# A row softmax on one core: the first of eight stores is issued from GpSimd instead of the Scalar engine

## The chip, the core and the metric

The kernel runs on one core of a Trainium2 chip. The metric is the device time of one execution in microseconds. Of the core's engines the kernel uses the vector engine (DVE), the scalar engine (ACT) and the queue of the sync engine (SP), which issues the loads. GpSimd (POOL) does only four small memsets at the start. Transfers between the chip's memory and the core's on-chip memory run on 16 DMA engines.

## The reference

The input is 16 x 1024 rows of 512 float32 values, 33.55 MB. Each row gets a softmax at temperature 0.5:

```python
temp = 0.5
x_scaled = x / temp
x_max = np.max(x_scaled, axis=-1, keepdims=True)
exp_x = np.exp(x_scaled - x_max)
return (exp_x / np.sum(exp_x, axis=-1, keepdims=True)).astype(np.float32)
```

The output has the same size, so 67.1 MB are moved in all.

## The kernel before

**Tiles.** The 16,384 rows are cut into 8 tiles (`c` = 0 to 7) of 128 partitions x 16 rows x 512 values, 4 MB each. The tile stays in place: it is loaded into an `xt` buffer, the exponentials and the scaled rows are written over it, and it is stored from there. There are 6 buffers (`BUFS`), so tiles 6 and 7 reuse those of tiles 0 and 1, and their loads wait until the stores of tiles 0 and 1 have landed.

**Blocks.** The work goes in blocks of rows of one tile: tile 0 has three (4, 4 and 8 rows), tiles 1 to 6 have one of 16 rows, tile 7 has two of 8. That makes 11 blocks, numbered 0 to 10.

**Steps of a block.**

- `shift` (loads L66, L74, L78): the tile's load is issued on SP's queue if that has not been done; DVE takes the negated maximum of each row (L74) and doubles it (L78) into `bias`.
- `exponentials` (L85): ACT computes exp(2x + bias) row by row and accumulates each row's sum.
- `scale_vector` (L100, L102): DVE takes the reciprocals of the sums and multiplies all but the last eighth of the block's rows.
- `scale_scalar` (L111): ACT scales the last eighth, one or two rows (none in the blocks of 4).
- `store` (L119): when the block is the last of its tile, one DMA of the whole tile, 4 MB, is issued.

**Order.** The schedule is written out by hand; every engine takes its instructions in the order of the program. The main loop runs over the blocks:

```python
shift(0)
shift(1)
exponentials(0)
for i in range(n):
    if i + 1 < n:
        exponentials(i + 1)
    scale_vector(i)
    scale_scalar(i)
    if i + 2 < n:
        shift(i + 2)
    store(i)
```

So on ACT the exponentials of the next block stand ahead of the last rows of this one, and the store's issue comes after both. All eight stores are issued on ACT's queue, and each waits for DVE's and ACT's rows of its tile. A new tile's load is issued within `shift`, in the order of tiles, on SP's queue; the load of tile 0 is split in two (1 MB and 3 MB).

Of the kernel before, what the change touches and what calls it, by code (L numbers as in the profile page):

```python
# [1 line left out]

# [4 lines left out]


@with_exitstack
def kernel(  # L10
    ctx: ExitStack,
    tc: tile.TileContext,
    x: bass.AP,
    out: bass.AP,
):
    nc = tc.nc
    fp32 = mybir.dt.float32
    P = nc.NUM_PARTITIONS
    AX = mybir.AxisListType.X
    EXP = mybir.ActivationFunctionType.Exp  # L20
    COPY = mybir.ActivationFunctionType.Copy
    MAX = mybir.AluOpType.max

    D = x.shape[-1]
    xf = x.flatten_outer_dims()
    of = out.flatten_outer_dims()
    N = xf.shape[0]

    G = 16
    C = N // (P * G)
    assert C * P * G == N
    xr = xf.rearrange("(c p g) d -> c p g d", p=P, g=G)
    outr = of.rearrange("(c p g) d -> c p g d", p=P, g=G)
    WHOLE = [(0, G)]
    LOADS = [[(0, 4), (4, G)]] + [WHOLE] * 7
    BLOCKS = [[(0, 4), (4, 8), (8, G)]] + [WHOLE] * 6 + [[(0, 8), (8, G)]]
    STORES = [WHOLE] * 8  # L40
    BMAX = 16
    BUFS = 6

    data = ctx.enter_context(tc.tile_pool(name="data", bufs=BUFS))
    stats = ctx.enter_context(tc.tile_pool(name="stats", bufs=6))

    ctx.enter_context(tc.manual_schedule())


    warm = stats.tile([P, 1], fp32, name="warm", bufs=1)  # L50
    nc.vector.memset(warm, 0.0)  # L51
    nc.scalar.activation(out=warm, in_=warm, func=EXP)  # L52

    chunks = {}
    blocks = [(c, lo, hi) for c in range(C) for lo, hi in BLOCKS[c]]
    n = len(blocks)
    biases, sums, recips = {}, {}, {}

    def load(c):
        if c < BUFS:  # L60
            chunks[c] = data.tile([P, G, D], fp32, name="xt")
        else:
            chunks[c] = chunks[c - BUFS]
        xt = chunks[c]
        for lo, hi in LOADS[c]:
            nc.sync.dma_start(out=xt[:, lo:hi, :], in_=xr[c][:, lo:hi, :])  # L66

    def shift(i):
        c, lo, hi = blocks[i]
        if c not in chunks:  # L70
            load(c)
        b = hi - lo
        negmax = stats.tile([P, BMAX], fp32, name="negmax")
        nc.vector.tensor_reduce(  # L74
            negmax[:, 0:b], chunks[c][:, lo:hi, :], axis=AX, op=MAX, negate=True
        )
        biases[i] = stats.tile([P, BMAX], fp32, name="bias")
        nc.vector.tensor_scalar_mul(biases[i][:, 0:b], negmax[:, 0:b], 2.0)  # L78

    def exponentials(i):  # L80
        c, lo, hi = blocks[i]
        sums[i] = stats.tile([P, BMAX], fp32, name="sums")
        for g in range(hi - lo):
            row = chunks[c][:, lo + g, :]
            nc.scalar.activation(  # L85
                out=row,
                in_=row,
                func=EXP,
                bias=biases[i][:, g : g + 1],
                scale=2.0,  # L90
                accum_out=sums[i][:, g : g + 1],
            )


    def scale_vector(i):
        c, lo, hi = blocks[i]
        b = hi - lo
        k = b - b // 8
        recips[i] = stats.tile([P, BMAX], fp32, name="recip")
        nc.vector.reciprocal(recips[i][:, 0:b], sums[i][:, 0:b])  # L100
        rows = chunks[c][:, lo : lo + k, :]
        nc.vector.tensor_mul(  # L102
            rows, rows, recips[i][:, 0:k].unsqueeze(2).broadcast_to((P, k, D))
        )

    def scale_scalar(i):
        c, lo, hi = blocks[i]
        b = hi - lo
        for g in range(b - b // 8, b):
            row = chunks[c][:, lo + g, :]  # L110
            nc.scalar.activation(  # L111
                out=row, in_=row, func=COPY, scale=recips[i][:, g : g + 1]
            )

    def store(i):
        c, _, end = blocks[i]
        for lo, hi in STORES[c]:
            if hi == end:
                nc.scalar.dma_start(  # L119
                    out=outr[c][:, lo:hi, :], in_=chunks[c][:, lo:hi, :]  # L120
                )

    shift(0)
    shift(1)
# [11 lines that stand above are left out]
# [1 line left out]
_INS = ['x']  # L137
_OUTS = [((16, 1024, 512), 'float32')]


# [23 lines left out]
```

## Time and profile before

| what | value |
|---|---|
| median of 4 runs | 162.4 us (162.32 to 162.69) |
| the profiled execution's own time | 162.43 us |
| its span, first to last instruction | 160.7 us |
| DVE busy | 134.6 us (84%) |
| ACT busy | 102.1 us (64%) |
| POOL busy | 0.2 us, four memsets |
| bytes moved | 67.13 MB, mean 418 GB/s |
| store, issue to landing | 12.4 to 32.4 us, median 22.9 |
| load of 4 MB, median issue to landing | 30.0 us |

The span is what the profiler saw of the program's instructions; the rest of the execution's time lies before and after it. Times inside the profile count from the start of the span. "L74" is line 74 of the kernel file. In the rows of busy tenths, the span is cut into 40 slices of 4 us, and a digit is the busy share of a slice. The page's q1 is the queue of the loads (issued by SP) and q10 that of the stores (issued by ACT). "ACTq" and "SPq" are those engines' queues of issues, which are not counted as busy time. An issue only starts a transfer; the landing is when its data has arrived.

### The profile page before, as it was taken

Reading aid. Unit: us, or ns where it says so; the run is one execution under the profiler, and the core shown is the slowest. Engines: PE = TensorE matmul, PEld = TensorE weight load, DVE = VectorE, ACT = ScalarE, POOL = GpSimd, SP = SyncE. Lnnn points to the kernel's source line nnn. Section 1 sums busy time; section 2 is a strip of 40 time slices with the busy share of each in tenths; the row PEclk is TensorE's granted clock in tenths of the full one; section 3 lists DMA queues with packets and bytes.
Section 4 is the critical chain, followed back from the end, with each engine's and each line's share of the span. In section 5 each row is a group of like instructions: output and inputs, shape, how many; then the busy total and the mean of one; then the engine's idle time right before and its main releaser. Section 6 shows DMA issues by size and latency. Waiting matters only on the chain.

```text
span 160.7 us, 402 instructions
## 1 busy us (share of the span) xinstructions
DVE 134.6 (84%) x45; ACT 102.1 (64%) x273; POOL 0.2 (0%) x4
## 2 busy tenths in 40 slices
DVE  0608999999999999999999999999999999956000
ACT  3072549069979963997299909990999890790000
POOL 0000000000000000000000000000000000000000
DMA  5999999999999999999999999999999999999993
GB/s 196 457 457 457 392 424 490 392 400 508 392 400 392 392 498 408 400 465 441 400 457 449 400 441 467 392 441 473 392 408 506 392 392 514 400 392 514 400 392 139
DMA packets 2450, 67.13 MB, mean 418 GB/s; under 512 B 272, under 2 KB 272, under 8 KB 272
## 3 DMA queue, kind: packets, MB, share of 16 engines
q1 hardware_dynamic: 1296, 33.56, 49.2%
q10 hardware_dynamic: 1152, 33.55, 48.4%
q14 instruction: 2, 0.02, 0.0%
HBM read 33.55 MB, written 33.55 MB: 418 GB/s over the span
## 4 chain that ended last, share of the span: by engine, by line
DVE 80%; DMA 7%; ACT 4%; issue 0%; SPq 0%
DVE negmax L74 42%; DVE xt L102 36%; DMA xt<-in_x_dram 7%; ACT xt L85 4%; DVE bias L78 1%; DVE recip L100 1%; SPq L66 0%
## 5 line engine op out<-in xcount | busy, mean ns | idle before, releaser
L85 ACT ACTIVATE xt<-xt,bias 128x512 f32<-128x512 f32 x128 | 90.4, 707 | 41.6 <-DVE bias L78 41.1
L74 DVE TENSOR_REDUCE negmax<-xt 128x16 f32<-128x8192 f32 (+2 forms) x11 | 69.9, 6352 | 9.4 <-DMA xt<-in_x_dram 9.4
L102 DVE TENSOR_TENSOR xt<-xt,recip 128x7168 f32<-128x7168 f32 (+2 forms) x11 | 62.0, 5637 | 0.4
L85 ACT ACTIVATION_READ_ACCUMULATOR xt<-xt,bias 128x1 f32 x128 | 23.9, 186 | 0.0
L111 ACT ACTIVATE xt<-xt,recip 128x512 f32<-128x512 f32 x15 | 9.9, 705 | 0.0
L100 DVE RECIPROCAL recip<-sums 128x16 f32<-128x16 f32 (+2 forms) x11 | 2.4, 218 | 1.8 <-ACT xt L85 1.8
L78 DVE TENSOR_SCALAR bias<-negmax 128x16 f32<-128x16 f32 (+2 forms) x11 | 1.9, 173 | 0.4
L52 ACT ACT_TABLE_LOAD x1 | 1.3, 1283 | 0.7 <-PEq L148 0.7
L51 DVE MEMSET warm<- 128x1 f32 x1 | 0.1, 59 | 0.8 <-PEq L148 0.8
L52 ACT ACTIVATE warm<-warm 128x1 f32<-128x1 f32 x1 | 0.2, 203 | 0.0
L148 POOL MEMSET const-uint8-127<- 128x1 uint8 x1 | 0.1, 103 | 0.0
L148 POOL MEMSET const-bfloat16-1.0<- 128x1 bf16 x1 | 0.1, 102 | 0.0
L148 POOL MEMSET const-float32-0.0<- 128x1 f32 x1 | 0.1, 99 | 0.2 <-issue 0.2
L148 POOL MEMSET const-float32-1.0<- 128x1 f32 x1 | 0.1, 99 | 0.0
## 6 DMA issues: line engine op xcount, KB each, us to landing
out_dram<-xt ACTq DMA_DIRECT2D x8, 4096.0 KB, 22.9
xt<-in_x_dram SPq DMA_DIRECT2D x7, 4096.0 KB, 30.0
xt<-in_x_dram SPq DMA_DIRECT2D x1, 3072.0 KB, 11.6
xt<-in_x_dram SPq DMA_DIRECT2D x1, 1024.0 KB, 4.7
```

Source lines behind the costliest of these rows:

```text
L51: nc.vector.memset(warm, 0.0)
L52: nc.scalar.activation(out=warm, in_=warm, func=EXP)
L74: nc.vector.tensor_reduce(negmax[:, 0:b], chunks[c][:, lo:hi, :], axis=AX, op=MAX, negate=True)
L78: nc.vector.tensor_scalar_mul(biases[i][:, 0:b], negmax[:, 0:b], 2.0)
L85: nc.scalar.activation(out=row, in_=row, func=EXP, bias=biases[i][:, g : g + 1], scale=2.0, accum_out=sums[i][:, g : g + 1],)
L100: nc.vector.reciprocal(recips[i][:, 0:b], sums[i][:, 0:b])
L102: nc.vector.tensor_mul(rows, rows, recips[i][:, 0:k].unsqueeze(2).broadcast_to((P, k, D)))
L111: nc.scalar.activation(out=row, in_=row, func=COPY, scale=recips[i][:, g : g + 1])
L148: nc = _bacc.Bacc("TRN2", target_bir_lowering=False, num_devices=1)
```

## The change

The store of tile 0 is issued by GpSimd; the stores of tiles 1 to 7 are issued by the scalar engine as before. The transfer, its size, what it waits for and what waits for it are the same.

```diff
         c, _, end = blocks[i]
         for lo, hi in STORES[c]:
             if hi == end:
-                nc.scalar.dma_start(
-                    out=outr[c][:, lo:hi, :], in_=chunks[c][:, lo:hi, :]
-                )
+                queue = nc.scalar if c else nc.gpsimd
+                queue.dma_start(out=outr[c][:, lo:hi, :], in_=chunks[c][:, lo:hi, :])
```

## The prediction

> **What bounds the kernel now.** I read the page first (span, busy rows, rates, queues), then the chain of waits, then the times around the first store and at the end. The page:
>
> ```profile
> span 160.7 us, 402 instructions
> DVE 134.6 (84%) x45; ACT 102.1 (64%) x273; POOL 0.2 (0%) x4
> ...
> DMA  5999999999999999999999999999999999999993
> GB/s 196 457 457 457 392 424 490 392 400 508 392 400 392 392 498 408 400 465 441 400 457 449 400 441 467 392 441 473 392 408 506 392 392 514 400 392 514 400 392 139
> ...
> q1 hardware_dynamic: 1296, 33.56, 49.2%
> q10 hardware_dynamic: 1152, 33.55, 48.4%
> q14 instruction: 2, 0.02, 0.0%
> ...
> DVE 80%; DMA 7%; ACT 4%; issue 0%; SPq 0%
> ```
>
> The chain puts 80% on DVE, and DVE's row shows few holes. But the DMA row is full from the second slice to the last but one, and the two data queues (q1 loads, q10 stores) together fill 97.6% of the sixteen engines' span. So there are two limits side by side. The DMA one: a 32,768 B packet takes 1.21 us in the packet records, on 16 engines 433 GB/s, and 67.11 MB at that rate is 155.0 us. The first packet starts at 2.13 and the last store lands at 159.8, 157.7 us later; only 2.7 us of that is not full-rate transfer.
>
> The timeline has the two issues that matter, the first and the last store, and the work beside them (columns: start, us, engine, line, operation):
>
> ```profile
> 44.69 0.71 ACT L111 ACTIVATE xt<-xt,recip 128x512 f32<-128x512 f32 x1
> 45.43 0.38 ACTq L119 DMA_DIRECT2D out_dram<-xt  x1
> 46.03 0.17 DVE L78 TENSOR_SCALAR bias<-negmax 128x16 f32<-128x16 f32 x1
> 46.11 0.24 DVE L100 RECIPROCAL recip<-sums 128x16 f32<-128x16 f32 x1
> 46.24 0.72 ACT L85 ACTIVATE xt<-xt,bias 128x512 f32<-128x512 f32 x1 [0.83 <-DVE bias L78]
> 46.39 7.62 DVE L102 TENSOR_TENSOR xt<-xt,recip 128x7168 f32<-128x7168 f32 x1
> ...
> 120.41 4.41 DVE L74 TENSOR_REDUCE negmax<-xt 128x8 f32<-128x4096 f32 x1
> ...
> 143.43 3.89 DVE L102 TENSOR_TENSOR xt<-xt,recip 128x3584 f32<-128x3584 f32 x1
> 147.40 0.34 ACTq L119 DMA_DIRECT2D out_dram<-xt  x1
> ```
>
> Call tile c's load Lc and its store Sc. S7 is issued at 147.40, when DVE and ACT are done, and takes 12.4 us to land (the shortest of the eight stores). It need not wait for DVE alone: S6, issued at 132.9, takes 17.2 us and lands at 150.1. In the packet records 15 engines finish S6 at 148.69 to 149.08 and start S7 within hundredths of a microsecond; the sixteenth runs 1.1 us behind the latest of them (two instruction fetches of 8 KB, the q14 row, went through an engine in mid-kernel; that it is this one is my reading). Eight packets of 1.21 us follow, so most engines end at 158.4 to 158.8 and the late one at 159.8. Two facts follow. S7 could be issued about 1.1 us later without moving the end. And since 147.40 plus at most 1.3 us is where S7's packets already begin, no time can be won on the 15 engines unless DVE ends earlier; what can be won is at most the 1.1 us of the late one.
>
> The waits of SP's queue show where the first store matters beyond itself:
>
> ```profile
> SPq L66 <- DMA out_dram<-xt: 75.3, 2, 56.4
> ```
>
> L6 and L7 reuse the buffers of tiles 0 and 1 and wait for S0 and S1 to land. L6 is issued at 69.22, just as S0 lands (45.43 + 23.7), L7 at 88.6 (58.88 + 29.6). L6 lands at 95.1 and L7 at 115.2. DVE wants L6 at 103.79 and L7 at 120.41: slack 8.7 and 5.2 us.
>
> **The change part by part.** *The issue leaves ACT.* It removes one issue of 0.38 us at 45.43. ACT next waits for the bias until 46.24 anyway, so the 0.43 us between 45.81 and 46.24 is idle before and longer after: gain 0. Without that cover it would be 0.38 us at most.
>
> *S0 is not ready earlier.* Its last input is ACT's own COPY of row 15, ending at 45.40, behind the sixteen exponentials of tile 1. GpSimd waits for that and for DVE's 37.40. POOL's row is four memsets at the start, so nothing queues behind its wait. Change in readiness: 0.
>
> *The start of S0.* On ACT's queue the issue is at 45.43, and S0's first packets run at 50.0 to 51.1, behind load packets already under way. No GpSimd transfer is in the trace. From below: no earlier than the same 50, since the data is ready at the same time. From above, by the nearest rows: if GpSimd could not write its work list while DVE streams, it would wait for the L102 that runs from 46.39 to 54.01, then need 1.4 us as the very first load does (issued 0.73, first packet 2.13), 55.4 to 56. I take 50 to 52, nearest to the existing stores, since no row shows an engine holding up a transfer. Here a rule speaks against the change. The Trainium skill, SBUF — State Buffer, "SBUF: two separate sides", warns that descriptors of a GpSimd DMA are written by GpSimd itself and starve while DVE runs an operation that takes both of its port pairs; its "Who interferes with whom" exempts a reduce, and a two-input multiply from all but GpSimd's reads. By the broad warning S0 would start at about 56, by the exemption at 50; the trace of before cannot say.
>
> Meanwhile L4 and L5 are queued, up to 75.8 at shared rate, so the engines are not idle in either case. The start alone costs 0.
>
> *How S0 shares the engines.* In the packet records an engine takes one load packet and one store packet in turn when both queues have work. After the change S0 has its own queue, and S1, issued at 58.88, no longer stands behind it: three queues take turns. At about 60.2 S0 has 4 of its 8 packets per engine left; these need 12 turns instead of 8, in which loads get 4 turns rather than the 6 of an even split. Loads fall two packets behind; at every second turn that is 3.6 to 4.8 us. L7 lands at 118.8 to 120.0, still before 120.41. If S0 starts at 56, it has about 7 packets left at 60.2 and lands near 79 to 80. L5 is in by then, and L6, which waits for S0, and L7 follow at half rate: 79.5 + 1.4 + 2 x 19.4 = 119.7, plus up to 2 us by which the last engine's load packets trail in mixed traffic: 121.7, a stall of 1.3 us. S1 meanwhile lands earlier than its 88.5 by as much as the loads lose: the same bytes move in another order, and S3 to S7 run back to back from about 120 as before.
>
> The Trainium skill's rule in DMA: Bandwidth & Descriptors, "Queues, rings and completion order", that an engine drains some 9 to 17 descriptors of one queue before it turns to the next, would let S0's whole share go in one go; S0 would land near 60, and the sum would be the same 0. The 1.21 us alternation in the records is what I go by.
>
> *The joining of a queue.* In the window from 45 to 50 us the rate is 321 GB/s: when S0 joined the loads, two load packets per engine took 1.44 and 1.72 us instead of 1.21, about 0.75 us lost once (1.3 us by the window). This is in the time already. Whether S1, joining as a third queue, loses it again is not in the trace: from 0 (mixed traffic runs at 437 GB/s from 60 to 110) to 0.75. I take 0, since packets are back to 1.21 us within two turns and the later reordering never slows them.
>
> *Around the span.* The profiled execution took 162.43 us against a span of 160.65: 1.78 us outside, 0.03 above the median of 162.4. A third queue's set-up would lie there; with two data queues in 1.78 us, at most 0.9. I take 0.
>
> Sum: 0 + 0 + 0 + 0 + 0, so 162.4 us.
>
> **The rivals.** *Loads come too late (slower).* One mechanism: L6 is issued when S0 lands, so a late or thinly served S0 delays L7 past 120.41, DVE stalls and S7 is issued later. It decides once L7 lands after about 121.5 (120.41 plus the 1.1 us that the end forgives). With S0 starting at 56 the stall is 1.3 us, at 58 to 60 about 2.4; the end moves by 0.2 to 1.3: 162.6 to 163.7. If GpSimd's packets are much smaller than 32 KB and get a turn each, S0 starves: with halves it lands near 85, L6 some 5 us late, and the time is about 169. For it: no cover but 5.2 us of slack. Against: the slack is larger than the even-turn shift.
>
> *The third queue costs its 0.75 us again, or a set-up (slower):* 162.4 + 0.75 = 163.15. For it: the engines have no idle time to absorb it. Against: no slow packet after 52 us.
>
> *The loss at the joining disappears (faster):* if GpSimd's transfer starts without the 0.75 us, only the late engine gains, 162.4 - 0.75 = 161.65; the S7 issue forbids more than 1.1. For it: that engine sets the end. Against: S1 would join next, with the same loss.
>
> *GpSimd's queue changes nothing but the name:* the forecast's time.
>
> **How the numbers follow.** About 0.2%, 0.33 us, is what a measurement of this kernel can tell from no change. No change: 0.42. Late loads 0.20, of which starved 0.07; third queue or set-up 0.22; together slower 0.42. Faster 0.16. The likeliest single case gives 162.4. Its own range is 162.1 to 162.8. The range for 8 in 10 reaches down to the faster rival, 161.6, and up to a joining loss and a stall together, 162.4 + 0.75 + 1.3 = 164.5; it leaves out the starved case and a few per cent at either end.
>
> **What would show it.** Right: a DMA row full throughout, S0's packets of 32 KB at 1.21 us under a third queue from 50 to 52, S1 landing before 88.5, L7 at 118 to 121, DVE's L74 at 120.4 without a DMA wait, S7 issued at 147.4. Wrong: a wait of L74 on a load after 100 us, S0 landing after 80, packets of another size, DVE's L102 longer than 7.62 us, or a slice near 60 us that falls as the one at 45 does.

## The result, and the profile after

The change takes 162.84 us in the median of 43 runs against 162.34 us in 63 runs of the kernel before. The ratio is 1.0036, with a 95% interval of 1.0024 to 1.0048, so it is slower by some 0.4%: more than the 0.2% that a measurement can tell from no change. (That ratio leaves out the three longest times, 165.24 to 165.47, which lie over 1.5% above the fastest, and is not the ratio of the two medians, 1.003; the granted clock was 1.00 in every run.)

The median hides the shape. 12 of the 43 single times are at or under 162.5 us, as fast as before (50 of 63 there), and 11 are above 163.6, which is the longest of before; the longest is 165.47. The profiled execution took 165.10 us and is one of these longest ones, so its profile shows the loss enlarged. A second profile of the same kernel, of an execution of 163.17 us, is used further down.

First the page of the change: span, DMA rows, queues, chain, and the landing of the store that was moved.

```profile
span 163.3 us, 402 instructions
...
DMA  5998898999998899899999999998999999989980
GB/s 193 449 514 385 385 514 385 449 449 387 506 385 369 385 441 457 385 489 401 393 489 401 425 465 387 441 457 385 473 425 401 489 393 433 465 385 385 409 385 16
...
q1 hardware_dynamic: 1296, 33.56, 48.6%
q10 hardware_dynamic: 1008, 29.36, 41.7%
q0 software_dynamic: 144, 4.19, 6.0%
...
DMA 45%; DVE 33%; ACT 11%; issue 1%; SPq 0%
...
out_dram<-xt POOLq DMA_DIRECT2D x1, 4096.0 KB, 30.6
```

GpSimd's store is a third data queue, q0, with 144 packets: 128 of 32,768 B and 16 small ones that report the end, just as each store on q10 has. The DMA row has eights where it had nines, and its last slice is 0 while the one before is 8: for the last stretch a single engine is moving data. DVE's share of the chain has fallen from 80% to 33%, as the chain now runs through the landing of the first store and the load behind it.

The timeline of the change, with the instructions that the prediction named (start, us, engine, line, operation, and in brackets the idle time before and what ended it):

```profile
45.54 0.66 POOL L120 DMA_DIRECT2D out_dram<-xt  x1 [45.09 <-ACT xt L111]
...
76.31 0.33 SPq L66 DMA_DIRECT2D xt<-in_x_dram  x1
...
121.37 4.42 DVE L74 TENSOR_REDUCE negmax<-xt 128x8 f32<-128x4096 f32 x1 [1.05 <-DMA xt<-in_x_dram]
...
148.38 0.34 ACTq L120 DMA_DIRECT2D out_dram<-xt  x1
```

S0 is issued at 45.54 and lands at 76.2, 7 us later than before. L6 waits for that and is issued at 76.31 instead of 69.22. L7 lands at 121.4 instead of 115.2, DVE waits 1.05 us for it, and S7 is issued 0.98 us later. That looks like a complete explanation, and it is not the one that sets the end here. In the packet records S6 ends at 148.7 to 149.1 on 13 engines, at 150.3 to 150.4 on two and at 152.8 on one; before, it was 148.7 to 149.1 on 15 and 150.2 on the last. (Packet times in this document lie 0.4 us behind the trace's own; so set, they meet the times at which each engine's share is reported as landed. The records do not name a packet's engine: that is inferred from which packet starts where another ends, and it is a guess where several end together.) The late engine is still busy with S6 when S7 is issued, starts S7 without a gap, and ends at 162.5, while thirteen of the others stand idle for 0.4 to 1.1 us before S7. The others end at 159.3 to 160.1. The span grew by 2.6 us, and the late engine ends 2.6 to 2.7 us later.

Where do engines lose time? A packet of 32 KB takes 1.21 us when nothing disturbs it, one of 24, 16 or 8 KB 0.91, 0.61 or 0.31. I add up all that packets take above this and divide by the 16 engines: slow-packet time, a mean per engine, from the packet records of each profile. From 44 to 53 us, where S0 starts beside the loads, it is 0.83 before and 0.91 after; but the slowest single packet is 0.75 us too long before, and 1.92 and 1.89 after, on two engines. From 53 to 70, where S1 joins as the third queue, it is 0.06 before and 0.10 after, where nearly all of the excess is two packets, 0.80 and 0.17 us too long; I take them to be the late engine's. From 70 to 118 it is 0.14 before and 0.38 after, and about two thirds of the difference lies, as far as the engines can be told apart, on the three that are out of step.

### The profile page after: what moved, and what is told of

Same layout as the page of the kernel before. It is cut to its first block, busy times and chain, and to the rows that moved or that the text cites. A ratio compares the mean times of both kernels' runs of the same rounds, so it can differ in the third digit from the quotient of the medians.

```text
span 163.3 us, 402 instructions
## 1 busy us (share of the span) xinstructions
DVE 134.7 (82%) x45; ACT 102.1 (63%) x273; POOL 0.9 (1%) x5
## 4 chain that ended last, share of the span: by engine, by line
DMA 45%; DVE 33%; ACT 11%; issue 1%; SPq 0%
DMA xt<-in_x_dram 29%; DVE negmax L74 20%; DMA out_dram<-xt 16%; DVE xt L102 12%; ACT xt L85 10%; ACT xt L111 1%; DVE bias L78 1%; DVE recip L100 0%; SPq L66 0%
## 5 line engine op out<-in xcount | busy, mean ns | idle before, releaser
L74 DVE TENSOR_REDUCE negmax<-xt 128x16 f32<-128x8192 f32 (+2 forms) x11 | 69.9, 6353 | 10.3 <-DMA xt<-in_x_dram 10.3
L102 DVE TENSOR_TENSOR xt<-xt,recip 128x7168 f32<-128x7168 f32 (+2 forms) x11 | 62.0, 5637 | 0.4
L111 ACT ACTIVATE xt<-xt,recip 128x512 f32<-128x512 f32 x15 | 9.9, 707 | 0.0
L120 POOL DMA_DIRECT2D out_dram<-xt x1 | 0.7, 657 | 45.1 <-ACT xt L111 45.1
```

Source lines behind the costliest of these rows:

```text
L74: nc.vector.tensor_reduce(negmax[:, 0:b], chunks[c][:, lo:hi, :], axis=AX, op=MAX, negate=True)
L102: nc.vector.tensor_mul(rows, rows, recips[i][:, 0:k].unsqueeze(2).broadcast_to((P, k, D)))
L111: nc.scalar.activation(out=row, in_=row, func=COPY, scale=recips[i][:, g : g + 1])
L120: queue.dma_start(out=outr[c][:, lo:hi, :], in_=chunks[c][:, lo:hi, :])
```

## The experiments

Three theories were set against each other. A: three queues at work at once cost the engines time. B: the start from GpSimd's queue is itself costlier, and reaches the engines unevenly. C: the load of tile 7 comes too late, DVE waits, and the last store is issued late. All times below are medians, each compared with the kernel before on the same chip.

**e1, tile 1's store held back until tile 2's.** The edit to the changed kernel's main loop:

```diff
-        store(i)
+        if i == 4:
+            store(3)
+        if i != 3:
+            store(i)
```

> The store of tile 0 stays on GpSimd's queue, but the store of tile 1 is issued together with that of tile 2, near 75.5 us instead of 58.9, so that loads, GpSimd's store and the scalar queue's stores are never all three under way while tile 0's store runs (it landed at 72.4 to 76.2). Theory A, three queues at once: the turn order of the late engine is disturbed only when tile 1's store joins as a third queue, so this kernel falls back to the time of before, 162.2 to 162.5, with single times within 0.4 us of each other. Theory B, the software queue itself (its work list reaches the 16 engines unevenly, two of them lost 1.9 us and not 0.8 at the joining): the time stays near the change's median of 162.84, with single times from 162.2 up to 164 or more. Theory C, loads too late: tile 7's load waits for tile 1's store, so it would land after 120 us here too and the time is 163 or more.

It took 164.39 us (164.10 to 164.50, ratio 1.0127, 1.0114 to 1.0140). S1 was issued at 70.79, not near 75.5 with S2 as expected, but S0 had all but landed by then (71.1), so three queues hardly met. Only C's number, 163 or more, fits, and for another reason: DVE did not wait for a late load (two waits on loads, 9.4 us, both at the start). The windows of the profile (DVE, ACT, POOL busy time, clock, DMA share, GB/s) show where it went:

```profile
65.00:70.00 5.00, 5.00 (x1) 5.00 (x17) 0.00 (x0) 1.00 1.05 452
70.00:75.00 5.00, 5.00 (x2) 5.00 (x15) 0.00 (x0) 1.00 0.96 341
75.00:80.00 5.00, 4.93 (x4) 0.99 (x2) 0.00 (x0) 1.00 0.89 367
```

The rate dips here as it dips when S0 starts. Slow-packet time is 1.06 at S0's start, 1.12 from 70 to 82, where the scalar queue starts and L6 (issued at 71.28) right behind it, and 0.62 from 82 to 97: 1.74 us on top of one start, against 2.13 us more time. The 0.62 lies almost wholly at 89.9 to 92, where the scalar queue passes from S1 to S2; no transfer was issued then, so a start does not explain it. A queue that starts while another streams can cost each engine about 1 us.

**e5, the same with tile 0's store on the scalar queue.** The edit of e1 on the kernel before.

> The store of tile 1 issued late as in e1_s1_later, but tile 0's store on the scalar queue: the control that tells what GpSimd's queue costs when three queues never meet. In e1 slow packets appeared at three places where a direction of transfer started again beside the other (0.9 to 1.1 us per engine at 45 to 52 us, 1.1 at 70 to 80, 0.55 at 90 to 95). Theory A, three queues at once are what costs: GpSimd costs nothing in e1, so this kernel takes the same 164.1 to 164.5. Theory B, GpSimd's queue starts the engines unevenly: this kernel is faster than e1 by 0.3 to 0.6 us, 163.7 to 164.0, and its slow packets at 45 to 52 us sum to 0.82 per engine with none over 0.9.

It took 164.21 us (163.50 to 164.86, ratio 1.0113, 1.0092 to 1.0133). The median lies in A's range, but its interval overlaps that of e1, so the two theories are not told apart by the time. The profile says what B said of the start: 0.84 us of slow packets from 44 to 53 us, none over 0.81, against 1.06 and 1.45 in e1. And it shows a restart by itself, without GpSimd: S0 had landed at 69.3, S1 was issued on the empty scalar queue at 70.78, and the slow-packet time from 70 to 82 is 0.97 us (0.03 before). The rate falls to 328 GB/s, from 426 in the same window before:

```profile
70.00:75.00 5.00, 5.00 (x2) 5.00 (x15) 0.00 (x0) 1.00 0.93 328
```

**e2, all stores on GpSimd's queue.**

```diff
-                queue = nc.scalar if c else nc.gpsimd
+                queue = nc.gpsimd
```

> All eight stores go through GpSimd's queue: again two data queues, loads and stores, as before the change, but the stores' queue is the software one. Theory A, three queues at once: as before the change, 162.2 to 162.6. Theory B, the software queue: at least as slow and as scattered as the change, 162.8 to 165, since every store reaches the engines unevenly. If the last store starts later from GpSimd than the 1.3 us of the scalar queue, up to 1.1 us of that is hidden by the late engine, the rest adds to either number.

162.74 us (162.56 to 163.51, ratio 1.0034, 1.0022 to 1.0046): as slow as the change with only two data queues, and without the scatter (no time of the nine is above 163.51). GpSimd's later issue of the last store (147.91) stood in the way of a clean reading, hence the next ones.

**e6, all but the last store on GpSimd's queue.** `queue = nc.gpsimd if c < 7 else nc.scalar`.

> Stores of tiles 0 to 6 through GpSimd's queue, the last one on the scalar queue. Against e2_all_gpsimd it takes away only GpSimd's later start of the last store (147.91 and some 1.5 us there, 147.40 and at most 1.3 us before). If the 0.48 us of e2 is that start, this kernel is back at 162.2 to 162.4. If it is the uneven start of the engines by the software queue (theory B), it stays at 162.6 to 162.9. Theory A, three queues at once, expects 162.2 to 162.4, as only two data queues work together.

163.18 us (162.79 to 163.38, ratio 1.0050, 1.0038 to 1.0062). Slower than e2, which neither theory expected. The last store now starts a queue of its own, and the slow-packet time after 118 us is 0.61 against 0.10 to 0.18 in kernels without such a start. The edit put one cost in the place of another, so it decides nothing.

**e9 and e10, the last store in two halves; all stores on the scalar queue, and all on GpSimd's.** The halves keep the engines supplied while the last issue is on its way. The line goes into the kernel before for e9, and into e2's kernel for e10:

```diff
-    STORES = [WHOLE] * 8
+    STORES = [WHOLE] * 7 + [[(0, 8), (8, G)]]
```

> The kernel before with the last store in two halves (rows 0 to 7 once their block is scaled, rows 8 to 15 at 147.4). The engines then have half a store queued when the last issue comes, so the time of that issue no longer matters up to some 4 us; a control for the next two. Every theory expects 162.1 to 162.5: the latest DMA engine has no idle time to give back, and the second half ends where the whole store ended.

> All stores on GpSimd's queue, the last one in two halves, so that GpSimd's later issue of the last store is covered by the half before it. Two data queues work at any time. Theory A, it takes three queues at once: equal to its control e9, 162.1 to 162.5. Theory B, GpSimd's queue starts the engines more unevenly and with more loss (0.9 to 1.2 us per engine at 45 to 53 us against 0.83 to 0.87 from the scalar queue, in the profiles so far): slower than e9 by 0.2 to 0.6 us.

e9: 162.35 us, ratio 1.0001 (0.9987 to 1.0014), the same as before. e10: 162.67 us, ratio 1.0025 (1.0011 to 1.0038). This is the cleanest pair: two queues in both, the same work, the last issue covered, and GpSimd's queue costs 0.3 us. In its profile (the longest of its twelve executions, 163.68 us) the mean slow-packet time at the start is 0.92 us against 0.89 in e9, hardly more, but two packets are 1.7 us too long where e9 has none over 0.84, and the last engine ends at 160.8 instead of 159.6. After the start the two profiles hardly differ (0.15 and 0.14 us from 70 to 118). So B's price holds with two queues. That it is the unevenness that costs, as the slowest engine ends the kernel, is my reading of one long execution: whether the two long packets ran on the engine that ended last can't be told.

**e12, only the last store on GpSimd's queue.** `queue = nc.gpsimd if c == 7 else nc.scalar`.

> Only the last store through GpSimd's queue: its start by itself, with nothing behind it. In e2 GpSimd's issue came at 147.91 (0.5 us after the scalar queue's) and the packets of the last store some 1.5 us later; in e6 the last store, alone on its queue, slowed the packets beside it by 0.5 us per engine. Theory B expects both, 0.5 to 1.0 us on the engines that are not late and less than 1.0 in the time, 162.5 to 163.4. Theory A expects no cost of the queue as such, only the 0.5 us of issue of which the late engine hides up to 1.1: 162.2 to 162.5.

163.75 us (162.94 to 163.99, ratio 1.0081, 1.0061 to 1.0100): more than both, and above B's 163.4. The page gives the issue to landing of this store, the timeline its issue:

```profile
out_dram<-xt POOLq DMA_DIRECT2D x1, 4096.0 KB, 13.4
```

```profile
147.85 0.66 POOL L120 DMA_DIRECT2D out_dram<-xt  x1 [147.41 <-DVEq L158]
```

Issued 0.45 us later than S7 before and 1.0 us longer in landing (12.4 before). 15 engines end at 159.2 to 159.4, and the late engine, which ends S6 at 150.2 as before, ends at 161.2: it has a packet that is 1.40 us too long. The late engine's 1.1 us, which hides a delay on the others, hides nothing when the late engine itself is hit.

**e4 and e11, the late load taken out of the way.** e4 loads tile 7 in halves, `LOADS = [[(0, 4), (4, G)]] + [WHOLE] * 6 + [[(0, 8), (8, G)]]`; e11 stores tile 7 in halves, as e9. Both on the changed kernel.

> The changed kernel with the load of tile 7 in two halves, so that the vector engine's reduce at 120.4 waits for its first half alone, which lands some 5 us earlier: the wait of 1.05 us seen in the profile of the change is gone. Theory C, the late load sets the time: back to 162.2 to 162.5. Theories A and B, the late DMA engine sets the time: the median stays near 162.8, single times up to 164 or more, and in the profile the last store is issued at 147.4 and yet one engine ends late.

> The changed kernel with the last store in two halves. A late vector engine can no longer leave the DMA engines idle at the end. Theory C, the late load of tile 7 and the vector engine's wait set the time: back to e9's 162.1 to 162.5. Theories A and B, the latest DMA engine sets it: median near 162.8, single times up to 164 or more, as the change.

e4: 163.28 us (162.14 to 165.36, ratio 1.0054, 1.0028 to 1.0081). e11: 163.20 us (162.54 to 164.54, ratio 1.0064, 1.0041 to 1.0088). Neither is faster than the change. The waits in e4's profile show that DVE's late wait is gone, with two waits left, both at the start:

```profile
DVE negmax L74 <- DMA xt<-in_x_dram: 9.6, 2, 4.8
```

C falls as the cause of this change's loss. e4's profile also happened on a short execution, 162.14 us, and shows what a harmless uneven start looks like: seven engines take up S0 at 50.6 to 51.2 us and nine some 1.6 us later, yet the 16 engines end within 0.7 us of each other, at 158.7 to 159.4.

**e3, only tile 3's store on GpSimd's queue.** `queue = nc.gpsimd if c == 3 else nc.scalar`.

> Only the store of tile 3 goes through GpSimd's queue, issued near 92 us while tile 2's store and the loads of tiles 6 and 7 run: three queues at once, but no load waits for tile 3's store. Theory A: slower and scattered as the change, 162.6 to 164, with a DMA engine that ends 2 to 3 us behind the others. Theory C, loads too late because tile 0's store lands late: no load is behind this store, tile 7's load falls at most two turns (2.4 to 4.8 us) back, to 118 to 120, and the time is that of before, 162.2 to 162.5. Theory B: slower by the same amount as the change.

165.70 us (165.04 to 167.48, ratio 1.0249, 1.0209 to 1.0289), outside every expectation. Here C is real, though nothing waits for this store:

```profile
124.29 4.42 DVE L74 TENSOR_REDUCE negmax<-xt 128x8 f32<-128x4096 f32 x1 [3.58 <-DMA xt<-in_x_dram]
...
151.30 0.34 ACTq L120 DMA_DIRECT2D out_dram<-xt  x1
```

The scalar queue (S2, then S4), S3 and the loads take turns while S3 runs, so loads get every third turn for 8 rounds; by my count that costs four load packets, 9.7 us at every second turn, and L7 lands 9.1 us later than before. DVE waits 3.58 us. S7 is issued 3.9 us late, and in the rate row of the page the slice at 148 us falls to 136 GB/s: the engines ran out of work. The slow-packet time is 0.05 from 82 to 97 us and 0.13 from 97 to 118 (0.04 and 0.07 before), so GpSimd's queue, started third, slowed almost nothing. The price of the share, not of the meeting, shows here; no run with the last store in halves tests it.

**e7, tiles 0 and 1 on GpSimd's queue.** `queue = nc.gpsimd if c < 2 else nc.scalar`.

> Stores of tiles 0 and 1 through GpSimd's queue, the rest on the scalar queue: the three queues now meet from 75.5 us, when tile 2's store is issued while tile 1's is under way until about 88, and no longer at 58.9. Tile 7's load is not behind tile 2's store. Theory A: scattered and slower as the change, single times 162.2 to 165, median 162.8 or more. Theory B: the uneven start at 45 to 52 us stays and the meeting of queues adds nothing: median 162.6 to 162.8 with little scatter, as e2.

162.83 us (162.16 to 164.52, ratio 1.0037, 1.0010 to 1.0064). The median fits both theories; the scatter is that of the change and speaks for A, against B.

**e8, the change again.** The kernel unaltered.

> The changed kernel itself, unaltered, for a second profile and more single times. Both theories expect a median near 162.84 and single times from 162.2 to 165; they differ in the profile if it falls on a typical execution: by theory B the engines' slow packets at 45 to 52 us are uneven (some over 1.0 us) and the last engine's store of tile 7 ends later than 159.9 by as much as that engine lost there; by theory A the slow packets of the last engine lie after 58.9 us.

162.86 us (162.13 to 163.63, ratio 1.0027, 1.0008 to 1.0046). In its profile, of an execution of 163.17 us, DVE has no wait for L7:

```profile
DVE negmax L74 <- DMA xt<-in_x_dram: 9.4, 2, 4.8
```

The slow-packet time is 0.96 from 44 to 53 us with a worst of 1.18, and 0.66 from 70 to 118 us against 0.14 before. The last engine ends at 160.5. So this execution, slower than the median, has no stall of DVE at all. Against before, 0.13 us more of slow packets lie at S0's start, and 0.52 us more after 70 us, well after S1 joined.

**e13 and e14, only tile 1's store on GpSimd's queue,** whole last store and in halves. `queue = nc.gpsimd if c == 1 else nc.scalar`. This has the three queues of the change from 59 us on, but S0 starts from the scalar queue.

> Only the store of tile 1 through GpSimd's queue. The first store still starts beside the loads from the scalar queue (0.83 to 0.94 us of slow packets per engine, none over 0.91, in five profiles), and three queues meet from 58.9 us as in the change, with the queues' roles swapped. If the meeting of three queues makes part of the change's cost (its single times reach 165.5 while two software-queue kernels stay under 163.7): median 162.6 or more, single times over 163.7. If the start from GpSimd's queue makes all of it: 162.1 to 162.5, as before the change, slow packets of 0.05 us per engine from 53 to 70 us.

> The same with the last store in two halves, so that a wait of the vector engine on tile 7's load cannot leave the DMA engines idle at the end. If three queues cost engine time: equal to e13. If e13 is slow only because tile 7's load comes after 120.4 and the vector engine waits: back to 162.1 to 162.5.

e13: 164.09 us (164.07 to 164.11, ratio 1.0093, 1.0076 to 1.0110). e14: 164.30 us (162.70 to 164.70, ratio 1.0094, 1.0063 to 1.0126). The time alone would be put down to the meeting of three queues. The windows of e13 say otherwise:

```profile
60.00:70.00 10.00, 9.93 (x4) 7.18 (x21) 0.00 (x0) 1.00 1.08 465
...
80.00:85.00 5.00, 5.00 (x1) 5.00 (x16) 0.00 (x0) 1.00 1.10 413
85.00:90.00 5.00, 5.00 (x2) 5.00 (x16) 0.00 (x0) 1.00 0.80 321
```

Nothing is lost where the three meet (slow-packet time 0.04 from 53 to 70 us). The dip is at 82 to 97 us, with 1.03 us in e13 and 1.15 in e14, after S2 was issued on a scalar queue that had run empty at 71.5. It is a restart again, but of which queue is open: L6's first packets run at 78.5, S2's at 79.7 to 82.3. DVE waits on three loads in all, 11.7 us, in both, so the late load is there, and e14 shows that it is not what costs.

## Why the prediction was right or wrong

The measured 162.84 lies in the range of 161.6 to 164.5, but the likeliest case was no change, at 0.42, and the time moved. Point by point:

*Issue and readiness: right.* POOL's issue is at 45.54 and its wait ended with ACT's L111, as said; ACT gained nothing.

*The start of S0: right.* The first packets of q0 run at 50.6, within 50 to 52, while L102, a two-input multiply, runs from 46.23 to 53.85; the starvation did not occur. But GpSimd's issue, 45.54 to 46.19, had ended before L102 began, so this start is no test of the rule. In e2 the issue of tile 5's store lies within an L102 and takes 0.53 us, as those beside an L74 do:

```profile
125.26 7.63 DVE L102 TENSOR_TENSOR xt<-xt,recip 128x7168 f32<-128x7168 f32 x1
...
125.66 0.53 POOL L120 DMA_DIRECT2D out_dram<-xt  x1 [16.09 <-ACT xt L111]
```

The exemption in the Trainium skill, SBUF — State Buffer, "Who interferes with whom", agrees with this row.

*Turns: right, but for the late engines.* The three queues take one 32 KB packet each in turn. L7 lands at 118.4 to 118.9 on 15 engines; I had said 118.8 to 120.0. The last engine's share lands at 121.4, and in e8 at 120.6, and that share is what DVE waits for. S1 lands at 85.3, before 88.5. What I did not see is that the first store lands when its slowest engine does: 13 engines finish S0 at 72.4 to 72.7, one at 74.4 and two at 76.2.

*The joining of a queue: wrong, and this is the step that failed.* I wrote that the loss at S0's start "is in the time already", and priced only a second loss when S1 joins third, at 0 to 0.75, taking 0. The third joining costs next to nothing: from 53 to 70 us 0.04 us per engine in e8, the same kernel, and in e13, and 0.10 in the long execution of the change. But the loss at S0's start is not the same from GpSimd. In the profiles with the start from the scalar queue (before, e3, e5, e9, e12, e13, e14) it is 0.80 to 0.94 us per engine with no packet more than 0.91 too long; in those with the start from GpSimd's (the change, e1, e2, e4, e6, e7, e8, e10, e11) it is 0.91 to 1.19, and the worst packet is 1.10 to 1.92 too long. The means differ by some 0.2 us; the spread differs more. e10 against e9 gives the price in the time with no third queue: 0.3 us, beside the 0.5 of the change. That does not make it the whole cause. The two-queue kernels are slower more evenly (2 of 12 times in e10 and none of 9 in e2 are at or under 162.5, against 12 of 43), and in e8 the start is the smaller part of the loss. The larger part, after 70 us, stood nowhere in the sum. The rival "the third queue costs its 0.75 us again" came nearest in size, at 163.15, with the wrong queue.

*The late engine's cushion of 1.1 us: right, and a likely reason why 12 of 43 executions are as fast as before.* A loss on the 15 others up to about 1.1 us need not show (e4's profile); a loss on the late one goes straight into the time (e12, and the change's profiled execution). I counted on it for a late S7 and did not ask what happens if the late engine itself is hit.

*The rival of the late load: real, not the cause.* The stall occurs in the long execution (1.05 us) and fully in e3. Removing it, in e4 and e11, gives nothing back.

**What stays open.** e8, e11 and the change have 0.38 to 0.66 us of slow packets from 70 to 118 us (0.14 before). Single times of the change, e4, e7 and e11, where three data queues meet in mid-kernel, reach 164.5 to 165.5, and those of the two-queue kernels e2 and e10 163.7 at most. In the change S0 lands so late that L6 is issued at 76.3 with L5's packets ending at 77.2; no load packet starts until 80.9, so the loads restart too. But e4 has the same gap with 0.13, and e5 and e13 differ in which restart costs. That starts and restarts of a queue beside a busy one come with 0 to 1.2 us of slow packets per engine is shown; what decides between them is not, and so the part of the scatter that is owed to three queues is not settled. No version here beats the kernel before; e9 equals it.

## What to carry to other kernels

Where DMA engines are full from end to end, moving a transfer to another queue isn't free even if its issue, its wait and its bytes are all hidden: ask how many times a queue starts from empty beside a busy one, and allow for each start a loss, here from nothing to about 1 us per engine. Read such a kernel by its slowest DMA engine and not by the mean, since a transfer lands and the kernel ends with that engine; a cushion that other engines have does not protect it. And take several single times before believing one profile: the long execution's stall of DVE was plain in the chain of waits, and two experiments that removed it gained nothing.

## What the runs showed of the hardware

GpSimd's first issue took 0.66 us and each later one 0.53 (e2), against 0.34 to 0.38 from the scalar queue. It issued the last store 0.55 to 0.59 us after DVE's last multiply had ended (e2, e10, e12), the scalar queue 0.08 to 0.09 us after. Three queues shared an engine packet by packet, one 32 KB packet each, with 0.04 to 0.10 us of slow packets per engine where the third joined (53 to 70 us in the change, e8 and e13). The same edit, one store on GpSimd's queue, cost 0.4% for tile 0, 0.9% for tile 1, 2.5% for tile 3 and 0.8% for tile 7, so the cost depends on which store is moved, and the queue by itself does not set it.
